# An eighth Strassen pair in each feed-forward layer, begun in the first half of the tokens

## The chip, the cores and the metric

The kernel runs on one core of one Trainium2 chip. The metric is the device time of one execution in microseconds (us); shorter is better. TensorE (PE) multiplies, VectorE (DVE) and ScalarE (ACT) do the element-wise work, GpSimd (POOL) does a little of it and issues transfers, and SyncE (SP) issues transfers only. PSUM, where PE accumulates, has eight banks of 128 partitions x 2 KB; one bank holds a 128 x 512 float32 tile.

## The reference

Two layers work on 512 tokens of width 1024. The first layer mixes tokens with causal average pooling, the second with causal differential attention. Each is followed by a SwiGLU feed-forward block (FFN) of width 2816. All arithmetic is float32.

```python
for i in range(DEPTH):                      # DEPTH = 2
    h = _multiscale_pool(x, ...) if i % 2 == 0 else _diff_attention(x, ...)
    x = _layernorm(ALPHA * x + h, ln_mix_g[i], ln_mix_b[i])
    x = _layernorm(ALPHA * x + _swiglu(x, w_gate[i], w_up[i], w_down[i]), ...)

def _swiglu(x, w_gate, w_up, w_down):
    return (jax.nn.silu(x @ w_gate) * (x @ w_up)) @ w_down
```

## The kernel before, in words

**A float32 product is three fast ones.** Each operand is split into a high part, a ScalarE cast to PE's faster type fp32r, and a low part, a VectorE subtraction of the high part from the value. PE then does high x high, high x low and low x high (`mm3`, lines 149 to 151). So each piece of weight costs a cast on ACT and a low part on DVE before PE can use it. x is kept transposed in `xt` as high and low parts: for each 128 tokens PE transposes (`pt`, line 235), ACT applies the norm's gain and bias and casts (lines 249 and 123), and DVE makes the low part (line 124). This is `turn(n, s)`, and it follows `norm(n, s)`, a short chain on DVE with one power on POOL (lines 183 to 208).

**Gate and up.** The 2816 columns are 22 blocks of 128. A weight row of the wall in DRAM is 128 x 1024 values, 512 KB, and gives one block of gate or of up. A plain block multiplies gate and up by all 1024 of x with 512 tokens as moving columns: 48 + 48 matmuls of 512 columns. The first `early` blocks (three in layer 0, two in layer 1) are computed in two token halves, 256 columns each, because the second half of x comes late: the loop over `lo = 0, 256` runs all early blocks for tokens 0 to 255, with the transposes of the last tokens between them (`late`), then all for tokens 256 to 511.

**Strassen pairs.** Blocks of number 2k and 2k+1 of this order are a pair k. The pairs of `SPLIT` (4 to 10) are done by Strassen's scheme in Winograd's form, two by two over gate/up and the halves of x and tokens: seven products of 24 matmuls with 256 columns (P1, Q5, P6, Q3, P7, P2, Q4) in place of eight. Their left sides are quarters of x and four sums of them (`xs`, made once per layer by `sums_of_x`, in steps called by `next(sums)`). Their right sides are four weight rows as they are or in sums of them (`sum` steps, line 636). The products go to three PSUM banks: A takes P1, P6, P7 and Q4 in one accumulation, C takes Q5 and Q3, B takes P2. After P1, ACT copies A's state to SBUF (`sg`); after P2, DVE adds bank B to it (line 925), and ACT applies Silu (line 932).

**What sets the order.** The order is written out by hand: each engine executes its instructions in the order of the code. `steps` lists cast, sum and low of each weight piece; `advance(upto)` and `ahead(upto)` emit steps until that piece is complete, a few pieces ahead of PE. Weight pieces lie in six slots of high and low part each (`w..h`/`w..l` or `g_..h`/`g_..l`) and start as raw rows in five buffers (`raws`), which SP fills in the order of the wall's rows. A slot is free when PE has done its last product on it. `weight_sums()` and `sum_hidden(k)` make sums for the down product, which is done by Strassen's scheme as well (lines 960 to 1000) and isn't touched. `ready(n)` emits cast and low of plain weight rows until n rows are ready, in and around attention.

Of the kernel before, what the change touches and what calls it, by code (L numbers as in the profile page):

```python
# [12 lines left out]
F32 = mybir.dt.float32  # L13
# [35 lines left out]
SPLIT = (4, 5, 6, 7, 8, 9, 10)  # L49
# [5 lines left out]
def trunk(ctx, tc, x, wall, pscale, lam_p, subln, table, lng, lnb, band, first, onehot, out):  # L55
# [37 lines left out]
    total = wall.shape[0]  # L93
    attn = 2 + 3 * FB
    vrow = {c: attn + 2 * c for c in range(4)}
    qrow = attn + 8
    order_of_rows = (
# [4 lines left out]
    rows_of_wall = list(range(total))  # L102
    rows_of_wall[attn : attn + 24] = order_of_rows
# [207 lines left out]
    with tc.tile_pool(name="pool", bufs=1) as pp:  # L311
# [198 lines left out]
        norm(0, 2)  # L510
        summed(3, 0, 1)
        spread_of(0, 3)
        ready(6)
# [19 lines left out]
    def ffn(layer, late):  # L533
# [3 lines left out]
        c1 = c0 + 2 * FB  # L537
        tt = nc.vector.tensor_tensor
        with tc.tile_pool(name=f"ffn{layer}", bufs=1) as fp:
# [12 lines left out]
            def block(i, b):  # L552

                if PAIRS[i][1] == 2:
                    return wall[c1 + 4 * i + b]
                return wall[c1 + 20 + b // 2][:, (b % 2) * 512 : (b % 2 + 1) * 512]
# [33 lines left out]
            chunks, index, steps = [], {}, []  # L590
# [7 lines left out]
            for k in range(HALF):  # L598
                j0 = index[k] = len(chunks)
                c = c0 + 4 * k  # L600
                if k in SPLIT:

                    chunks += [(c, ()), (c, (c, c + 1)), (c, (c, c + 2)), (c + 2, ())]
                    chunks += [(c + 1, (c + 1, c + 2)), (c + 3, ()), (c, (c, c + 3))]
                    step("cast", j0)
                    for w in (
                        "low 0, sum 1, cast 1, sum 4, cast 3, cast 4, low 1, sum 2, cast 2, low 3, "
                        "low 2, sum 6, cast 5, cast 6, low 4, low 5, low 6"
                    ).split(", "):
                        steps.append((w[:-2], j0 + int(w[-1])))  # L610
                else:
                    for i in range(4):
                        chunks.append((c + i, ()))
                        step("cast", j0 + i)
                        step("low", j0 + i)
# [115 lines left out]
            def load_terms(k):  # L731
                if k < HALF - 1:
                    c = c1 + 4 * (k // 2)
                    src = wall[c : c + 4][:, :, term_slice(k)].rearrange("(j r) p t -> p j r t", j=2)
                else:
                    src = wall[c1 + 20 : c1 + 22].rearrange("j p (r t) -> p j r t", r=2)
# [33 lines left out]
            def sum_hidden(k):  # L770

                first, second = hid[:, k, :256], hid[:, k, 256:]
                a12, a22 = hid[:, k + HALF, :256], hid[:, k + HALF, 256:]
                u = fp.tile([P, 2, 256], F32, tag="u", name=f"u{layer}_{k}", bufs=1)
                v = fp.tile([P, 2, 2, 256], F32R, tag="v", name=f"v{layer}_{k}", bufs=2)
# [7 lines left out]
                tt(v[:, :, 1, :], u, v[:, :, 0, :].bitcast(F32), op=ALU.subtract)  # L783
                yield
                nc.scalar.dma_start(out=ssum[:, :, :, k, :], in_=v.bitcast(F32))
# [41 lines left out]
            early = 3 if layer == 0 else 2  # L827
# [3 lines left out]
            sums = sums_of_x()  # L831
            ks = [range(4 * b, 4 * b + 4) for b in range(2)]
            by_part = [(0, 0, range(KB)), (0, 1, range(KB)), (1, 0, range(KB))]
            by_half = [(0, 0, ks[0]), (1, 0, ks[0]), (0, 0, ks[1]), (1, 0, ks[1])]
            by_half += [(0, 1, ks[1]), (0, 1, ks[0])]
            for lo in (0, 256):
                for f in range(early):
                    for i in range(2):
                        product(
                            accs[f][i], 2 * f + i, lo, lo + 256,  # L840
                            None if layer or lo else by_part if f or i else by_half,
                        )
                        if not lo and (f, i) in late:
                            late[f, i]()
                        if not lo:
                            advance(2 * early, True)
                    if lo:
                        advance(2 * f + 6)
                        gated(order[f], *accs[f])
                        affine(n - 1, f)  # L850
                        catch_up()
                        if f < 2:
                            weight_sums()
                            next(sums)
                        if f == 1:
                            behind.append(sum_hidden(0))

            def plain(f):
                k = f // 2
                j = index[k] + 2 * (f % 2)  # L860
# [10 lines left out]
                if f in (3, 5, 7):  # L871
                    weight_sums()
                if f == 3:
                    load_terms(3)
                if f % 2:
                    behind.append(sum_hidden(k))

            def strassen(k):
                names = {"P1": "A", "P6": "A", "P7": "A", "Q4": "A", "Q5": "C", "Q3": "C", "P2": "B"}
                banks = {b: bank(f"{b}{layer}_{k}") for b in "ACB"}  # L880
                lefts = {
                    "P1": [quarter(0, i, 0) for i in range(2)],
                    "P2": [quarter(0, i, 1) for i in range(2)],
                    "Q4": [quarter(1, i, 1) for i in range(2)],
                }
                for m, p in enumerate(("Q5", "P6", "P7", "Q3")):
                    lefts[p] = [xs[:, m, i] for i in range(2)]
# [3 lines left out]
                def both(t):  # L891
                    return t.rearrange("p (f t) -> p f t", f=2)
# [4 lines left out]
                for j, p in enumerate(GATE):  # L897
                    acc = banks[names[p]]
                    h, l = halves[index[k] + j]
                    xh, xl = lefts[p]  # L900
                    for f in range(2):
                        o = acc[:, f * 256 : (f + 1) * 256]
                        for kk in range(4):
                            c = slice((4 * f + kk) * P, (4 * f + kk + 1) * P)
                            for e, (w, x) in enumerate(((h, xh), (h, xl), (l, xh))):
                                nc.tensor.matmul(  # L906
                                    o, w[:, c], x[:, kk, :],
                                    start=p in ("P1", "Q5", "P2") and f + kk + e == 0,
                                    stop=p in ("Q4", "Q3", "P2") and (f, kk, e) == (1, 3, 2),
                                    skip_group_check=True,  # L910
                                )
# [17 lines left out]
                    ahead(index[k] + j + 6)  # L929
# [117 lines left out]
    def attention():  # L1047
        n = 2
        with tc.tile_pool(name="attn", bufs=1) as ap:
# [421 lines left out]
    ffn(0, {(1, 0): later(0, 2), (1, 1): later(0, 3)})  # L1471
# [110 lines left out]
```

## Time and profile before

| | us |
|---|---|
| median of 3 runs (939.54 to 940.16) | 939.98 |
| the profiled execution | 940.01 |
| its span on the core | 938.2 |
| PE busy | 925.0 |
| DVE busy | 789.8 |
| ACT busy | 512.9 |
| POOL busy | 126.7 |

The span runs from the first to the last instruction; times of rows are counted from its start. By the trace, x's first half is multiplied by the early blocks up to 52.0 us in layer 0, the second half from 52.0 to 69.3, plain blocks run to 123.7, Strassen pairs to 264.8 and the down product to 362.8. Attention follows to about 586. In layer 1 the early blocks' second half runs from 600.8 to 618.0, plain blocks to 683.3, and pairs to 824.5. In rows of instructions, a row has start, duration, engine, line, operation, out<-in, and in brackets the engine's idle time before it with what ended it.

### The profile page before, as it was taken

What the parts mean: (1) busy time and instruction counts of PE and PEld (TensorE: products, weight loads), DVE (VectorE), ACT (ScalarE), POOL (GpSimd) and SP (SyncE); (2) the same over time, 40 slices, a digit from 0 to 9 for tenths busy, and PEclk for the clock granted to TensorE, in tenths of its full rate; (3) what the DMA queues carried; (4) which work ended last, traced back from release to release, by engine and by line L of the source; (5) the groups of instructions that cost most, each with busy time, mean ns of one, the idle gap of its engine ahead of it and who ended that gap; (6) DMA issues with size and microseconds to landing.
All of it is one profiled execution on the core that took longest, in us unless ns stands there. A gap on an engine that the chain in (4) does not pass through costs nothing.

```text
span 938.2 us, 14939 instructions
## 1 busy us (share of the span) xinstructions
PE 925.0 (99%) x5710; PEld 827.2 (88%) x5710; DVE 789.8 (84%) x1166; ACT 512.9 (55%) x814; POOL 126.7 (14%) x152
## 2 busy tenths in 40 slices
PE   9999999999999999999999999999999999999996
PEld 8998899999988888888888887988899999988884
DVE  8969889999988778968888877788789999987678
ACT  6652444555564457667878754734245554654450
POOL 4221121110101201201112100211111110001101
PEclk9999999999999999999999999999999999999999
DMA  8487988886868988975666522597887885878942
GB/s 243 154 266 225 336 283 245 259 258 211 259 199 277 363 256 232 226 198 154 164 137 178 159 68 68 148 322 226 258 255 243 266 277 192 264 244 286 353 156 91
DMA packets 86038, 211.11 MB, mean 225 GB/s; under 512 B 15140, under 2 KB 26660, under 8 KB 85966
## 3 DMA queue, kind: packets, MB, share of 16 engines
q1 hardware_dynamic: 43420, 117.16, 38.1%
q0 software_dynamic: 18768, 58.20, 24.8%
q10 hardware_dynamic: 23778, 34.78, 10.4%
q8 instruction: 45, 0.74, 0.3%
q14 instruction: 27, 0.22, 0.1%
HBM read 173.40 MB, written 36.72 MB: 224 GB/s over the span
## 4 chain that ended last, share of the span: by engine, by line
PE 92%; DVE 5%; ACT 1%; issue 1%; DMA 0%; POOL 0%; DVEq 0%; ACTq 0%; POOLq 0%
PE A L906 17%; PE P L973 14%; PE C L906 9%; PE Q L973 6%; PE B L906 4%; PE g L150 3%; PE u L150 3%; PE g L149 3%; PE u L151 3%; PE u L149 3%; PE g L151 3%; PE s L1192 2%; PE va L1123 2%; PE wo L150 1%; PE wo L151 1%; PE q L149 1%
## 5 line engine op out<-in xcount | busy, mean ns | idle before, releaser
L636 DVE TENSOR_TENSOR raw<-raw,raw 128x1024 f32<-128x1024 f32 x56 | 68.3, 1219 | 0.5
L123 ACT CAST xs<-hid 128x512 fp32r<-128x512 f32 (+1 forms) x60 | 34.7, 581 | 24.4 <-DVE hid L813 24.4
L124 DVE TENSOR_TENSOR xs<-hid,xs 128x512 fp32r<-128x512 f32 (+1 forms) x60 | 38.5, 643 | 7.8 <-ACT xs L123 7.8
L1212 ACT ACTIVATE p<-p,mn 128x128 f32<-128x128 f32 (+3 forms) x64 | 35.2, 552 | 14.1 <-DVE mn L1207 14.1
L249 ACT ACTIVATE y<-pt,bT,gT 128x128 f32<-128x128 f32 x72 | 27.1, 456 | 26.6 <-PE pt L235 23.5
L744 POOL DMA_DIRECT2D b<-in_wall x20 | 14.0, 706 | 172.4 <-DMA tsum<-b 68.8
L805 POOL DMA_DIRECT2D xs<-ssum x24 | 17.4, 725 | 140.8 <-PE Q L973 67.8
L677 DVE TENSOR_TENSOR hid<-sg,u 128x512 f32<-128x512 f32 x16 | 11.0, 687 | 25.5 <-PE u L151 14.7
L199 POOL TENSOR_TENSOR rs<-rs,mhalf 128x1 f32<-128x1 f32 x16 | 12.8, 800 | 140.9 <-DVE rs L198 97.3
L744 POOL DMA_DIRECT2D hid<-in_wall x24 | 18.9, 831 | 77.5 <-DMA tsum<-hid 50.2
L1207 DVE CUSTOM_DVE_ANT_0 p<-s,bias 128x128 f32<-128x128 f32 (+3 forms) x64 | 28.0, 485 | 1.1 <-PE s L1192 1.1
L781 ACT CAST v<-u 128x512 fp32r<-128x512 f32 x22 | 13.7, 621 | 26.9 <-DVE u L779 26.8
L190 DVE BATCH_NORM_STATS2 st<-res 128x6 f32<-128x512 f32 x32 | 22.2, 694 | 1.1
L932 ACT ACTIVATE sg<-sg 128x512 f32<-128x512 f32 x14 | 8.9, 633 | 26.0 <-DVE sg L925 26.0
L745 POOL DMA_DIRECT2D hid<-in_wall x12 | 14.8, 1233 | 55.1 <-DMA hid<-in_wall 55.1
L693 ACT CAST xs<-hid 128x1024 fp32r<-128x1024 f32 x8 | 8.4, 1051 | 24.0 <-DVE hid L710 11.6
L124 DVE TENSOR_TENSOR xt<-y,xt 128x512 fp32r<-128x512 f32 x18 | 12.3, 691 | 10.9 <-ACT xt L123 10.7
L921 DVE TENSOR_TENSOR hid<-C,hid 128x512 f32<-128x512 f32 x14 | 9.7, 691 | 10.7 <-PE C L906 9.2
L1226 DVE SCALAR_TENSOR_TENSOR p<-p,sm,p 128x128 f32<-128x128 f32 (+3 forms) x32 | 17.6, 551 | 1.1
L917 ACT COPY hid<-C 128x512 f32<-128x512 f32 x14 | 8.2, 588 | 18.2 <-PE C L906 18.2
L124 POOL TENSOR_TENSOR sql<-sq,sqh 128x512 fp32r<-128x512 f32 x7 | 9.3, 1324 | 60.5 <-ACT sqh L123 60.5
L745 POOL DMA_DIRECT2D b<-in_wall x10 | 12.3, 1230 | 38.0 <-DMA b<-in_wall 38.0
(1211 smaller groups left out, 3637.1 us busy)
## 6 DMA issues: line engine op xcount, KB each, us to landing
raw<-in_wall SPq DMA_DIRECT2D x122, 512.0 KB, 5.0
r<-tsum SPq DMA_DIRECT2D x40, 512.0 KB, 4.5
hid<-in_wall POOLq DMA_DIRECT2D x36, 512.0 KB, 7.3
b<-in_wall POOLq DMA_DIRECT2D x30, 512.0 KB, 5.8
r<-in_wall SPq DMA_DIRECT2D x30, 512.0 KB, 4.5
tsum<-hid ACTq DMA_DIRECT2D x24, 512.0 KB, 5.4
ssum<-v ACTq DMA_DIRECT2D x22, 512.0 KB, 3.8
tsum<-b ACTq DMA_DIRECT2D x20, 512.0 KB, 4.9
```

The source lines that it names most:

```text
L123: nc.scalar.copy(dst_h, src)
L124: (low or nc.vector).tensor_tensor(dst_l, src, dst_h.bitcast(F32), op=ALU.subtract)
L149: nc.tensor.matmul(acc, ah, bh, start=start, stop=False)
L150: nc.tensor.matmul(acc, ah, bl, start=False, stop=False)
L151: nc.tensor.matmul(acc, al, bh, start=False, stop=stop)
L249: nc.scalar.activation(y[:, k, :], pt[:, k * P : (k + 1) * P], AF.Identity, bias=bT[:, n, kk : kk + 1], scale=gT[:, n, kk : kk + 1],)
L636: tt(t, raws[pair[0]], raws[pair[1]], op=ALU.add)
L744: nc.gpsimd.dma_start(out=t[:, j], in_=src[:, j])
L906: nc.tensor.matmul(o, w[:, c], x[:, kk, :], start=p in ("P1", "Q5", "P2") and f + kk + e == 0, stop=p in ("Q4", "Q3", "P2") and (f, kk, e) ...
L973: nc.tensor.matmul(accs[s], x[:, k, r], y[:, c], start=first and k == 0 and e == 0, stop=last and k == m - 1 and e == 2, skip_group_check= ...
L1207: nc.vector.tensor_tensor_reduce(out=p, in0=accs[c], in1=biases[h][:, w - 1 :: -1] if w < S else biases[h][:, ::-1], op0=ALU.add, op1=ALU. ...
L1212: nc.scalar.activation(p, p, AF.Exp, bias=mn[:, q, c : c + 1], scale=-1.0, accum_out=sm[:, q, c : c + 1],)
```

## The change

`SPLIT` gains pair 3, so that eight pairs are done by Strassen's scheme. `EARLY` is two blocks in layer 0 (three before) and one in layer 1 (two before). In the first token half, P1 and P2 of pair 3, which need only tokens 0 to 255, follow the early blocks; ACT copies P1 from bank A into a tile `g3`, and DVE adds bank B to it. Two rows of the wall, `pair` and `pair + 3`, are loaded early for this, and once more later for the pair's sums: two more loads of 512 KB per layer. Bank B is held for the whole layer. In later pairs ACT copies P1 from bank A into bank B, and P2 accumulates on it; the DVE addition is gone and Silu reads bank B. Further: one buffer `v` instead of two; `weight_sums` at other places; w5 is made ready ahead of the last norm of layer 0's mixer; the transpose of tokens 384 to 511 comes after P1 (after block 1's up before); the second half's first gate product of layer 0 takes x in halves; and in attention's end a `ready` stands ahead of `scaled(last)`.

```diff
-SPLIT = (4, 5, 6, 7, 8, 9, 10)
+SPLIT = (3, 4, 5, 6, 7, 8, 9, 10)
+EARLY = (2, 1)
...
+    def rows_of_ffn(layer, c):
+        g = list(range(c, c + 2 * FB))
+        e, pair = 2 * EARLY[layer], c + 4 * SPLIT[0]
+        return g[:e] + [pair, pair + 3] + g[e:] + list(range(c + 2 * FB, c + 3 * FB))
...
         norm(0, 2)
+        ready(6)
         summed(3, 0, 1)
         spread_of(0, 3)
-        ready(6)
         norm(0, 3)
...
+            def half_product(acc, j, left, start, stop):
+                h, l = halves[j]
+                xh, xl = left
+                for f in range(2):
+                    o = acc[:, f * 256 : (f + 1) * 256]
+                    for kk in range(4):
+                        c = slice((4 * f + kk) * P, (4 * f + kk + 1) * P)
+                        for e, (w, x) in enumerate(((h, xh), (h, xl), (l, xh))):
+                            nc.tensor.matmul(
+                                o, w[:, c], x[:, kk, :],
+                                start=start and f + kk + e == 0,
...
+            halved = [(w, e, ks[b]) for b in range(2) for w, e in ((0, 0), (1, 0), (0, 1))]
...
             for lo in (0, 256):
                 for f in range(early):
                     for i in range(2):
...
                     if lo:
-                        advance(2 * f + 6)
+                        advance(2 * f + 8)
                         gated(order[f], *accs[f])
                         affine(n - 1, f)
                         catch_up()
-                        if f < 2:
-                            weight_sums()
-                            next(sums)
+                        weight_sums()
                         if f == 1:
                             behind.append(sum_hidden(0))
+                if not lo:
+                    bankA, bankB = bank(f"A{layer}_{SPLIT[0]}"), bank(f"B{layer}")
+                    half_product(bankA, number[SPLIT[0], 0, "pair"], lefts["P1"], True, False)
+                    if "P1" in late:
+                        late["P1"]()
+                    nc.scalar.copy(both(g3), both(bankA))
+                    next(sums)
+                    half_product(bankB, number[SPLIT[0], 5, "pair"], lefts["P2"], True, True)
+                    tt(both(g3), both(bankB), both(g3), op=ALU.add)
+                    next(sums)
...
                     if p == "P1":
-                        g0 = tile_of(0)
-                        nc.scalar.copy(both(g0), acc)
+                        nc.scalar.copy(both(bankB), acc)
...
                     elif p == "P2":
-                        tt(both(g0), acc, both(g0), op=ALU.add)
+                        g0 = tile_of(0)
...
                     if p == "P2":
-                        nc.scalar.activation(g0, g0, AF.Silu)
+                        nc.scalar.activation(both(g0), acc, AF.Silu)
...
             for s in range(SB):
                 acc = gather(0, s, ws, between[s])
-                if s in (0, 3):
-                    scaled(last - 1 if s == 0 else last)
+                if s == 0:
+                    scaled(last - 1)
                 ready(cw + min(5 + s, WBUFS) if s < 3 else cw + 8)
+                if s == 3:
+                    scaled(last)
...
-    ffn(0, {(1, 0): later(0, 2), (1, 1): later(0, 3)})
+    ffn(0, {(1, 0): later(0, 2), "P1": later(0, 3)})
```

Three places show how it moves instructions. The first is the first token half of layer 0. On PE before, `u_1` (block 1's up) is followed by the transposes of the last 128 tokens and block 2 (`g_2`, `u_2`), whose weights are the pieces `g_4` and `g_5`; the high part's 16 matmuls come ahead of the low part's eight:

```order
L659 MATMUL u_1_538<-xt,w5h 128x256 x16
L659 MATMUL u_1_538<-xt,w5l 128x256 x8
L235 MATMUL pt_3_0_679<-ident,res 128x128 x4
L235 MATMUL pt_3_1_680<-ident,res 128x128 x4
L659 MATMUL g_2_539<-xt,g_4h 128x256 x16
L659 MATMUL g_2_539<-xt,g_4l 128x256 x8
```

On PE now, P1 of pair 3 (`A_3`) stands in the place of `g_2` and ahead of the transposes:

```order
L683 MATMUL u_1_538<-xt,w5h 128x256 x16
L683 MATMUL u_1_538<-xt,w5l 128x256 x8
L867 MATMUL A_3_678<-xt,g_4h 128x256 x2
L867 MATMUL A_3_678<-xt,g_4l 128x256
L867 MATMUL A_3_678<-xt,g_4h 128x256 x2
```

The last two lines go on by turns, 24 matmuls in all; then come the transposes and P2 (`B_679`, from `g_5`). The low part of `g_4` is wanted at the third matmul, where it was wanted at the seventeenth.

On DVE at the same place before, `w5l` stands behind the last tokens' sums, and `g_4l` behind their norm:

```order
L124 TENSOR_TENSOR w4l<-raw_326,w4h 128x1024
L208 TENSOR_SCALAR res<-res,mv_2_492,rs_2_494 128x1024
L183 SCALAR_TENSOR_TENSOR res<-res,mix_0_400 128x512
L190 BN_STATS st_3_505<-res 128x6
L183 SCALAR_TENSOR_TENSOR res<-res,mix_1_401 128x512
L190 BN_STATS st_3_505<-res 128x6
L196 BN_AGGR mv_3_509<-st_3_505 128x2
L198 TENSOR_SCALAR rs_3_511<-mv_3_509 128x1
L124 TENSOR_TENSOR w5l<-raw_328,w5h 128x1024
L208 TENSOR_SCALAR res<-res,mv_3_509,rs_3_511 128x1024
L642 TENSOR_TENSOR g_4l<-raw_330,g_4h 128x1024
```

On DVE now:

```order
L133 TENSOR_TENSOR w4l<-raw_326,w4h 128x1024
L217 TENSOR_SCALAR res<-res,mv_2_492,rs_2_494 128x1024
L133 TENSOR_TENSOR w5l<-raw_328,w5h 128x1024
L192 SCALAR_TENSOR_TENSOR res<-res,mix_0_400 128x512
L199 BN_STATS st_3_511<-res 128x6
L192 SCALAR_TENSOR_TENSOR res<-res,mix_1_401 128x512
L199 BN_STATS st_3_511<-res 128x6
L205 BN_AGGR mv_3_515<-st_3_511 128x2
L207 TENSOR_SCALAR rs_3_517<-mv_3_515 128x1
L217 TENSOR_SCALAR res<-res,mv_3_515,rs_3_517 128x1024
L666 TENSOR_TENSOR g_4l<-raw_330,g_4h 128x1024
```

`w5l` has moved ahead of the sums, and all from the sums to `g_4l` behind it.

The second place is ACT after the last transposed tokens of layer 0 (`y_3_1`). Before, the table of Silu is loaded and the first Silu (`sg_0`, block 0's gate) stands ahead of the casts of the next weights:

```order
L123 CAST xt<-y_3_1_696 128x4x128
L676 ACT_TABLE_LOAD
L676 ACTIVATE sg_0_799<-g_0_535 128x512
L639 CAST g_6h<-raw_497 128x1024
L639 CAST g_7h<-raw_514 128x1024
L639 CAST g_8h<-raw_571 128x1024
L676 ACTIVATE sg_11_870<-g_1_537 128x512
```

Now:

```order
L132 CAST xt<-y_3_1_721 128x4x128
L915 COPY g_0_545<-A_3_678 128x512
L663 CAST g_6h<-raw_497 128x1024
L663 CAST g_7h<-raw_504 128x1024
L663 CAST g_8h<-raw_570 128x1024
L700 ACT_TABLE_LOAD
L700 ACTIVATE sg_0_819<-g_0_535 128x512
```

The copy of P1 and three casts now stand ahead of the first Silu.

The third place is the end of attention on DVE, where the last head's output is scaled (`rso`, then its low part into `xt`) and the output product's weights are made. Before:

```order
L183 SCALAR_TENSOR_TENSOR res<-res,wo_2_0_5792 128x512
L183 SCALAR_TENSOR_TENSOR res<-res,wo_2_1_5793 128x512
L1277 SCALAR_TENSOR_TENSOR rso_5856<-o_5812,gcol,rso_5856 128x512
L124 TENSOR_TENSOR xt<-rso_5856,xt 128x512
L124 TENSOR_TENSOR w98l<-raw_5518,w98h 128x1024
L124 TENSOR_TENSOR w99l<-raw_5650,w99h 128x1024
```

Now, where all numbers of weights are two higher:

```order
L192 SCALAR_TENSOR_TENSOR res<-res,wo_2_0_5827 128x512
L192 SCALAR_TENSOR_TENSOR res<-res,wo_2_1_5828 128x512
L133 TENSOR_TENSOR w100l<-raw_5553,w100h 128x1024
L133 TENSOR_TENSOR w101l<-raw_5685,w101h 128x1024
L1327 SCALAR_TENSOR_TENSOR rso_5891<-o_5847,gcol,rso_5891 128x512
L133 TENSOR_TENSOR xt<-rso_5891,xt 128x512
```

Two weights' low parts stand ahead of the scaling instead of behind it.

More of the change, by code (lines that the diff above doesn't have):

```diff
@@ L92, in trunk @@
     divided = [0]
-    total = wall.shape[0]
     attn = 2 + 3 * FB
@@ L536, in ffn @@
         c0 = base[0]
-        c1 = c0 + 2 * FB
+        c1 = c0 + 2 * FB + 2
+        down = rows_of_wall[c0] + 2 * FB
+        early = EARLY[layer]
         tt = nc.vector.tensor_tensor
@@ L596, in step, with plain_chunk @@
                     steps.append((kind, j))
[L598 to L615, printed above, removed]
+            def plain_chunk(key, c):
+                number[key] = len(chunks)
+                chunks.append((c, ()))
+                step("cast", number[key])
+                step("low", number[key])
@@ L835, in ffn @@
             by_half += [(0, 1, ks[1]), (0, 1, ks[0])]
+            halved = [(w, e, ks[b]) for b in range(2) for w, e in ((0, 0), (1, 0), (0, 1))]
+            g3 = fp.tile([P, S], F32, name=f"g3_{layer}")
+            ready_first = 2 * early + 2
             for lo in (0, 256):
@@ L879, in strassen @@
                 names = {"P1": "A", "P6": "A", "P7": "A", "Q4": "A", "Q5": "C", "Q3": "C", "P2": "B"}
[L880 to L887, printed above, removed]
+                begun = k == SPLIT[0]
@@ L888, in strassen @@
+                banks = {"A": bankA if begun else bank(f"A{layer}_{k}"), "C": bank(f"C{layer}_{k}")}
+                banks["B"] = bankB
                 rows = hid[:, k : k + HALF + 1 : HALF, :]
                 first, second = rows[:, :, :256], rows[:, :, 256:]
-                def both(t):
-                    return t.rearrange("p (f t) -> p f t", f=2)
                 def tile_of(i):
                     return keep.tile([P, S], F32, tag="y", name=f"sg{layer}_{k}_{i}", bufs=2)
-                for j, p in enumerate(GATE):
-                    acc = banks[names[p]]
[L899 to L911, printed above, removed]
@@ new lines, in strassen @@
+                for m, p in enumerate(GATE):
+                    if begun and p in ("P1", "P2"):
+                        if p == "P2":
+                            g0 = g3
+                            nc.scalar.activation(g0, g0, AF.Silu)
+                        continue
+                    acc = banks[names[p]]
+                    j = number[k, m, "pair"]
+                    half_product(
+                        acc, j, lefts[p], p in ("P1", "Q5"), p in ("Q4", "Q3", "P2")
+                    )
```

74 lines of the change are left out of this document (57 added, 17 removed).

## The prediction

> **What bounds the kernel now.** The page comes first: the span, the engines' busy time, and the chain that ended last.
>
> ```profile
> span 938.2 us, 14939 instructions
> PE 925.0 (99%) x5710; PEld 827.2 (88%) x5710; DVE 789.8 (84%) x1166; ACT 512.9 (55%) x814; POOL 126.7 (14%) x152
> ```
>
> PE is busy 925.0 of 938.2 us. So the time is PE's work plus what makes it wait. The next view is PE's waits, with total, count and longest.
>
> ```profile
> PE u L659 <- DVE w5l L124: 0.8, 1, 0.8
> PE wo L150 <- DVE w98l L124: 0.7, 1, 0.7
> PE pt L235 <- DVE res L208: 0.2, 1, 0.2
> ```
>
> Two of these lie where the change acts. No wait on a DMA is listed. The windows by stage come third: length, then busy time of PE, weight load, DVE, ACT and POOL, granted clock, DMA share, GB/s.
>
> ```profile
> 46.00:52.00 6.00, 6.00 (x53) 6.00 (x52) 3.23 (x5) 3.91 (x10) 0.00 (x0) 1.00 0.98 355
> 52.00:69.20 17.20, 17.20 (x146) 17.20 (x145) 11.40 (x12) 8.25 (x10) 5.41 (x6) 1.00 0.85 230
> 69.20:123.70 54.50, 54.50 (x243) 45.12 (x243) 48.13 (x56) 18.42 (x22) 9.34 (x10) 1.00 0.85 279
> 143.90:264.80 120.90, 120.90 (x1009) 120.90 (x1009) 114.36 (x140) 63.65 (x82) 10.45 (x12) 1.00 0.79 248
> 600.00:623.00 23.00, 23.00 (x174) 22.12 (x173) 15.93 (x17) 12.54 (x19) 5.42 (x6) 1.00 0.99 305
> 925.00:930.00 5.00, 4.19 (x19) 3.14 (x17) 5.00 (x9) 0.00 (x0) 0.67 (x1) 1.00 0.28 105
> 930.00:938.20 8.20, 0.00 (x0) 0.00 (x0) 4.21 (x8) 0.00 (x0) 0.92 (x1) 0.73 0.35 129
> ```
>
> PE fills every stage of the FFN. DVE has 5.80 us idle in the second row and 6.37 in the third, 12.2 together, and only 5% in the pairs (fourth). The sum is made against the profiled execution's 940.01 us, which is 0.03 above the median.
>
> **1. PE's work.** The chain of waits gives the matmuls' prices (start, us, what).
>
> ```profile
> 49.13 2.88 PE u L659 x24
> 52.01 0.12 PE g L149
> 69.29 0.23 PE g L149
> 123.72 2.87 PE A L906 x24
> ```
>
> From 52.01 to 69.29 lie six products of 24 matmuls with 256 columns: 17.28 / 144 = 0.120 us each. From 69.29 to 123.72 lie 240 with 512 columns: 0.2268 each. In layer 0, 288 + 240 matmuls stand ahead of pair 4. Afterwards: two early blocks in halves (192 small), two plain blocks (192 large), pair 3 (168 small). That is 72 small more and 48 large fewer: 8.64 - 10.89 = -2.25 us. Layer 1 goes from 192 + 288 to 264 + 240, the same -2.25. Together **-4.5**.
>
> The Trainium skill, page "TensorE: Matmul & The Clock Gate", section "Back-to-back issue gap", gives N / 2.4 + 2.5 ns for a warm gap, which is 109 and 216 ns here. The trace has 120 and 227, about 11 ns above it at both sizes. By the page each layer would gain 2.50, and the sum would end 0.5 lower; the rows decide.
>
> **2. Layer 0, first token half.** DVE's and PE's timelines round the wait on `w5l` (start, duration; in brackets the idle time before and its cause):
>
> ```profile
> 39.50 0.68 DVE L183 SCALAR_TENSOR_TENSOR res<-res,mix 128x512 f32<-128x512 f32 x1
> 42.58 1.23 DVE L124 TENSOR_TENSOR w5l<-raw,w5h 128x1024 fp32r<-128x1024 f32 x1
> 44.24 0.81 DVE L208 TENSOR_SCALAR res<-res,mv,rs 128x1024 f32<-128x1024 f32 x1 [0.44 <-POOL rs L199]
> 44.97 1.22 DVE L642 TENSOR_TENSOR g_4l<-raw,g_4h 128x1024 fp32r<-128x1024 f32 x1
> 46.11 1.22 DVE L642 TENSOR_TENSOR g_5l<-raw,g_5h 128x1024 fp32r<-128x1024 f32 x1
> ```
> ```profile
> 40.87 2.15 PE L659 MATMUL u<-xt,w5h 128*128 128x256 f32 x16
> 43.86 1.21 PE L659 MATMUL u<-xt,w5l 128*128 128x256 f32 x8 [0.83 <-DVE w5l L124]
> 45.20 1.06 PE L235 MATMUL pt<-ident,res 128*128 128x128 f32 x8
> 46.02 1.19 PE L659 MATMUL g<-xt,g_4h 128*128 128x256 f32 x8
> ```
>
> `w5l` moves to 39.50, so u runs unstalled from 40.87 to 43.75. What stood there comes one low part later, 46.11 - 44.97 = 1.14: the norm at 45.38, `g_4l` from 46.11 to 47.33. P1 follows u at once, does two matmuls and waits at the third for `g_4l`, from 43.99 to 47.37, 3.38 us. Before, `g_4l` was covered by transposes and 16 high matmuls. P1's other 22 end at 50.01, the transposes (45.20 to 46.02) 0.82 later, P2 at 53.71. The second half, at 52.01 before, so starts 1.70 later, and layer 0 keeps -2.25 + 1.70 = **-0.55**. Within P1 the stall lies between 0 (`g_4l` there when P1 starts) and 3.38 plus the 1.14 of one more low part.
>
> The last tokens' x is next in line, since its transposes now follow P1. Before, from ACT's first operation on them to DVE's last low part it took 52.28 + 0.69 - 48.03 = 4.94 us:
>
> ```profile
> 48.03 1.51 ACT L249 ACTIVATE y<-pt,bT,gT 128x128 f32<-128x128 f32 x4 [3.09 <-DVE xt L124]
> 52.28 0.69 DVE L124 TENSOR_TENSOR xt<-y,xt 128x512 fp32r<-128x512 f32 x1 [1.37 <-ACT xt L123]
> ```
>
> With the first transposes done at 50.4 the last low part is there at about 55.4. The second half's first product now takes x in halves, the low part of the second half in its last four matmuls, at 53.71 + 20 x 0.12 = 56.1. So it is in time by 0.7 us, and I count zero for it; one more half-size DVE operation ahead of it (0.60) would still cost nothing.
>
> **3. VectorE up to the end of pair 3 in layer 0.** The new work is three more low parts (pair 3 has seven pieces for four), four sums, and about four half-size operations (bank B to `g3`, Q3, P7, a product more), less Silu's partner products. Prices by start-to-start times:
>
> ```profile
> 102.73 1.22 DVE L696 TENSOR_TENSOR xs<-hid,xs 128x1024 fp32r<-128x1024 f32 x1
> 103.86 0.69 DVE L783 TENSOR_TENSOR v<-u,v 128x512 fp32r<-128x512 f32 x1
> 104.46 1.22 DVE L642 TENSOR_TENSOR g_15l<-raw,g_15h 128x1024 fp32r<-128x1024 f32 x1
> ```
>
> Large operations take 1.14, half-size 0.60. 7 x 1.14 + 4 x 0.60 = 10.4 us, against the 12.2 idle. It fits with 1.8 us over, if the idle time can be used. Its largest piece before, and ACT at that time:
>
> ```profile
> 57.87 0.69 DVE L677 TENSOR_TENSOR hid<-sg,u 128x512 f32<-128x512 f32 x1 [4.90 <-PE u L151]
> ```
> ```profile
> 54.93 0.60 ACT L676 ACTIVATE sg<-g 128x512 f32<-128x512 f32 x1 [1.39 <-PE g L151]
> 55.43 1.04 ACT L639 CAST g_6h<-raw 128x1024 fp32r<-128x1024 f32 x1
> 57.69 1.05 ACT L639 CAST g_7h<-raw 128x1024 fp32r<-128x1024 f32 x1 [1.23 <-PE u L150]
> ```
>
> The 4.90 was spent waiting for block 0's up while the casts waited for PE to free slots. Now casts of `g_6` and `g_7` stand ahead of the first Silu, in the slots that P1 and P2 free at 50.01 and 53.71. Their low parts fill that hole. Cost **0**, with bounds 0 and +2.7 (rival A). If Q3's weight is the tight one, the margin is that 1.8.
>
> **4. Attention's end.** PE waits there for `w98l`:
>
> ```profile
> 567.08 0.75 DVE L1277 SCALAR_TENSOR_TENSOR rso<-o,gcol,rso 128x512 f32<-128x512 f32 x1 [2.67 <-ACT rso L1272]
> 568.52 0.69 DVE L124 TENSOR_TENSOR xt<-rso,xt 128x512 fp32r<-128x512 f32 x1 [0.69 <-ACT xt L123]
> 569.60 0.40 PE L149 MATMUL wo<-w98h,xt 128*128 128x512 f32 x1
> 570.75 0.50 PE L150 MATMUL wo<-w98l,xt 128*128 128x512 f32 x1 [0.75 <-DVE w98l L124]
> ```
>
> Two matmuls 1.15 apart instead of 0.227: 0.92 lost. Two low parts moved into DVE's 2.67 us of idle time take 2.28 and remove that wait. The scaled head is next in line: its low part in `xt` was there at 568.52 + 0.69 = 569.2, and the first matmul on it is at 569.60. The 0.2 that a later transpose waits for the norm grows a little as PE comes earlier, 0.15 by my estimate. **-0.75**, bounds -0.92 and 0 (casts too late on ACT, so that rso slips).
>
> **5. Layer 1.** P1 and P2 take the place of block 1's halves, with the same 48 matmuls and two weights made by a cast and a low part, in the same order. No wait is listed there before. DVE's idle time is 7.07 us from 600 to 623, and 11.9 in the plain blocks behind it:
>
> ```profile
> 623.00:683.30 60.30, 60.30 (x269) 49.93 (x268) 48.41 (x57) 20.05 (x24) 9.34 (x10) 1.00 0.82 253
> ```
>
> That is 19.0 against the same 10.4, where layer 0 has 12.2. The gain of -2.25 stays; its bounds are 0 and +2.7 as in layer 0, with 0 nearer by that slack.
>
> **6. Bank B, the other moves.** In 14 later pairs DVE loses one addition of 0.69, ACT's copy goes to PSUM instead of SBUF. DVE isn't on the path in the pairs (no wait listed), so nothing is gained. No row shows a copy by ACT into PSUM; the nearest is its copy from PSUM into SBUF, 0.588 us:
>
> ```profile
> L917 ACT COPY hid<-C 128x512 f32<-128x512 f32 x14 | 8.2, 588 | 18.2 <-PE C L906 18.2
> ```
>
> P2 wants the bank only after the four products Q5, P6, Q3 and P7, which take 11.5 us (2.88 each), so that even a copy ten times as long would be hidden.
>
> Holding bank B takes a bank from the plain blocks, whose five others turn over once in 2.5 blocks of 21.8 us / 2. One buffer `v` for two is asked for once per pair, 20 us. The four more row loads are rival B. If DVE got late in the pairs, the 0.69 taken off per pair would bring it back: 8 x 0.69 over a layer. All of these count zero.
>
> **Sum.** -0.55 (layer 0) - 0.75 (attention) - 2.25 (layer 1) = -3.55: **936.5 us**.
>
> **Rivals.** A: VectorE is late at pair 3. If the hole of 4.90 us can't be filled, since slots come free too late, 10.4 meets 7.3, and Q3 waits some 2.7 in layer 0 and perhaps a little in layer 1: 939.2, no change that can be told. For it: DVE is at 95% in the pairs and can't catch up. Against it: the casts' new place. Chance 0.18.
>
> B, slower: loads become the bound. Each layer reads 1.05 MB more, and right behind the early blocks, where the DMA share is 0.98 to 0.99. At 305 GB/s that is 3.4 us per layer, 6.9 in all: 943.4. Against it: no wait of PE names a DMA, and casts were released by PE. It decides where a raw row lands after its slot is free. Chance 0.14.
>
> C: the clock. The stall of 3.38 us is PE's longest. In this trace the granted clock falls only at the end: PE's last work ends at about 929.2, and the clock is still 1.00 in the window to 930 and 0.73 in that of 8.20 us behind it, so half speed for at most 4.4 us (0.27 x 8.2 x 2) from about 933.8, 4.6 us after. A fall at P1 would double the matmuls until it rises; if for as long as the stall, half of 3.38 us, +1.7: 938.2; two such windows 939.9. The Trainium skill's page named above, section "Part 1: The HAM clock gate (the "warmup" mystery)", says that a free-running idle window of about 3.4 us throttles PE to half; by that rule P1 is on the edge, while the trace's one fall came later. Chance 0.08.
>
> D: P1 doesn't stall much, -1.7 to -3.4 more, about 934.0. That `g_4l` is wanted at P1's third matmul speaks against it. Chance 0.10.
>
> **How the numbers follow.** My case has 0.50 and 936.5. About 0.2%, 1.9 us, is what can be told from no change: faster lies below 938.1, slower above 941.9. Faster: my case 0.47, D 0.10, C 0.03, A 0.05 = 0.65. Same: A 0.11, C 0.05, my case 0.03 = 0.19. Slower: B 0.14 and a heavy A 0.02 = 0.16. The range leaves out half of B and of D and goes from 934.5 to 942.0.
>
> **What would show it.** Right: PE waits once at P1's third matmul, about 3.4 us, on `g_4l`; none on `w5l` or the output product's weight; the second half of layer 0 starts at about 53.7, pair 4's P1 at 123.2 (A, line 906 before); 0.2 at most on weights in pair 3. Wrong: a wait at Q3 or P6 of pair 3 on DVE (A), waits of casts on DMA (B), a granted clock under 1.0 before 60 us (C), a span shorter still with no wait on `g_4l` (D), or a wait in the pairs for the copy into bank B, which the sum leaves out.

## The result and the profile after

The changed kernel takes 954.77 us (median of 5 runs, 954.43 to 955.83) against 939.98 before: ratio 1.0158, 95% interval 1.0145 to 1.0172. It is slower by 14.8 us where 3.5 less were forecast. The profiled execution took 954.77 us. The page's first lines and the waits of PE that bear on the change:

```profile
span 953.0 us, 15072 instructions
PE 925.6 (97%) x5758; PEld 831.5 (87%) x5758; DVE 801.3 (84%) x1172; ACT 521.2 (55%) x826; POOL 126.1 (13%) x152
```
```profile
PE A L867 <- DVE hid L973: 14.7, 2, 7.3
PE A L867 <- DVE g_4l L666: 2.3, 1, 2.3
PE pt L244 <- DVE res L217: 0.2, 1, 0.2
```

The first row is new: twice, once in each layer, PE waits 7.3 us at bank A for VectorE's line 973. That line is `tt(second, second, acc, op=ALU.subtract)`, VectorE's read of bank A after P7. The waits on `w5l` and on the output product's weight are gone. PE's busy time should have fallen by the work saved, yet it rose by 0.6: a busy PE isn't PE at full speed. The windows behind the three waits show the granted clock (third number from the end, ahead of DMA share and GB/s):

```profile
46.60:49.90 3.30, 3.30 (x15) 3.30 (x16) 2.25 (x3) 0.00 (x0) 0.45 (x1) 0.51 0.92 297
49.90:53.30 3.40, 3.40 (x32) 3.40 (x31) 0.00 (x0) 1.89 (x5) 2.27 (x3) 1.00 1.00 322
128.60:132.60 4.00, 4.00 (x22) 4.00 (x23) 2.76 (x3) 0.57 (x1) 0.00 (x0) 0.60 0.91 274
693.90:698.30 4.40, 4.37 (x20) 4.38 (x21) 2.84 (x3) 0.63 (x1) 0.02 (x1) 0.50 0.98 309
```

After each of them the clock was at 0.50 to 0.60 for 3.3 to 4.4 us; the second row shows it back at 1.00. The places in time come from the chain of waits. Before:

```profile
586.67 0.97 PE pt L235 x8
824.45 14.99 PE P L973 x66
```

After:

```profile
46.57 4.34 PE A L867 x22
51.78 2.87 PE B L867 x24
128.55 7.43 PE A L867 x48
135.98 2.88 PE C L867 x24
595.10 0.94 PE pt L244 x8
693.93 7.97 PE A L867 x48
840.14 14.99 PE P L1023 x66
```

Layer 0's second token half starts at 54.65 (51.78 + 2.87) instead of 52.01: +2.64. Pair 4's P1, the second half of the 48 matmuls from 128.55, starts at 133.10 (135.98 - 2.88) instead of 123.72: +9.38. Attention's last transposes stand at +8.43, so attention won back 0.95. The down product of layer 1 stands at +15.69, so layer 1 lost 7.26. The tail gives back 0.9, and the span is 14.8 longer. In parts:

| | layer 0 | layer 1 |
|---|---|---|
| PE's work, as forecast | -2.25 | -2.25 |
| P1's stall, less the stalls it replaces (what remains of +2.64) | +0.94 | |
| half clock behind it: 22 matmuls in 4.34, not 2.64 | +1.70 | |
| wait at Q4 for the read of P7 | +7.33 | +7.33 |
| half clock behind it: 48 matmuls, not 5.76 | +1.67 | +2.21 |
| sum (measured) | +9.39 (+9.38) | +7.29 (+7.26) |

Why the read is late is seen on PE and DVE around it in layer 0:

```profile
120.94 0.28 PE L867 MATMUL A<-xs,g_17l 128*128 128x256 f32 x1
128.55 0.80 PE L867 MATMUL A<-xt,g_18h 128*128 128x256 f32 x2 [7.33 <-DVE hid L973]
```
```profile
119.55 2.48 DVE L660 TENSOR_TENSOR raw<-raw,raw 128x1024 f32<-128x1024 f32 x2
121.95 1.22 DVE L666 TENSOR_TENSOR g_20l<-raw,g_20h 128x1024 fp32r<-128x1024 f32 x1
123.08 0.68 DVE L971 TENSOR_TENSOR hid<-C,hid 128x512 f32<-128x512 f32 x1
123.69 1.22 DVE L660 TENSOR_TENSOR raw<-raw,raw 128x1024 f32<-128x1024 f32 x1
124.82 1.22 DVE L666 TENSOR_TENSOR g_22l<-raw,g_22h 128x1024 fp32r<-128x1024 f32 x1
126.06 1.23 DVE L666 TENSOR_TENSOR g_21l<-raw,g_21h 128x1024 fp32r<-128x1024 f32 x1
127.21 0.68 DVE L807 TENSOR_TENSOR v<-u,v 128x512 fp32r<-128x512 f32 x1
127.81 0.68 DVE L973 TENSOR_TENSOR hid<-hid,A 128x512 f32<-128x512 f32 x1
```

P7 ends at 121.2. Its read stands in VectorE's queue behind sums and low parts of pair 4 (`g_20` to `g_22`), which PE wants only later, and comes at 127.81. Q4 accumulates on the same bank A, so it must not start before the read. In all other pairs P2 stands between P7 and Q4 and gives the read 2.88 us; in pair 3 P2 was done in the first token half.

### The profile page after: what moved, and what is told of

Same layout as the page of the kernel before. It is cut to its first block, busy times and chain, and to the rows that moved or that the text cites. A ratio compares the mean times of both kernels' runs of the same rounds, so it can differ in the third digit from the quotient of the medians.

```text
span 953.0 us, 15072 instructions
## 1 busy us (share of the span) xinstructions
PE 925.6 (97%) x5758; PEld 831.5 (87%) x5758; DVE 801.3 (84%) x1172; ACT 521.2 (55%) x826; POOL 126.1 (13%) x152
## 4 chain that ended last, share of the span: by engine, by line
PE 82%; DVE 12%; issue 3%; ACT 2%; DMA 0%; POOL 0%; DVEq 0%; ACTq 0%; POOLq 0%
PE A L867 19%; PE P L1023 13%; PE C L867 8%; PE Q L1023 6%; PE B L867 5%; PE va L1173 2%; PE s L1242 2%; PE q L158 2%; PE q L160 2%; PE k L158 2%; PE k L160 2%; PE q L159 2%; PE k L159 2%; DVE raw L660 2%; PE vc L1173 1%
## 5 line engine op out<-in xcount | busy, mean ns | idle before, releaser
L660 DVE TENSOR_TENSOR raw<-raw,raw 128x1024 f32<-128x1024 f32 x64 | 78.1, 1221 | 1.0
L768 POOL DMA_DIRECT2D b<-in_wall x20 | 14.0, 706 | 183.7 <-DMA tsum<-b 122.5
L867 PE MATMUL A<-xt,g_18h 128*128 128x256 f32 x32 | 9.3, 392 | 14.7 <-DVE hid L973 14.7
L978 ACT ACTIVATE sg<-A 128x512 f32<-128x512 f32 x16 | 9.6, 597 | 24.9 <-PE A L867 24.9
L867 PEld LDWEIGHTS A<-xt,g_18h 128*128 128x128 f32 x32 | 7.7, 294 | 15.1 <-DVE hid L973 15.1
L769 POOL DMA_DIRECT2D hid<-in_wall x12 | 14.8, 1233 | 41.8 <-DMA hid<-in_wall 41.8
L701 DVE TENSOR_TENSOR hid<-sg,u 128x512 f32<-128x512 f32 x12 | 8.2, 684 | 12.5 <-PE u L160 7.3
```

The costliest lines, as they stand in the source:

```text
L660: tt(t, raws[pair[0]], raws[pair[1]], op=ALU.add)
L867: nc.tensor.matmul(o, w[:, c], x[:, kk, :], start=start and f + kk + e == 0, stop=stop and (f, kk, e) == (1, 3, 2), skip_group_check=True,)
```

## The experiments

Two theories were held against each other. Theory 1, order: P2 is missing between P7 and Q4, and the read queues behind steps for later products. Theory 2, amount: VectorE has more to do up to pair 4 than fits, so that whatever order is mended, the wait shows elsewhere.

**Reads first** (the first kernel). In pair 3 the steps behind P6 and Q3 are put off until behind P7.

```diff
+                late_steps = [0]
...
+                    if begun and p in ('P6', 'Q3'):
+                        late_steps[0] += 1
+                        continue
                     ahead(j + 6)
-                    catch_up()
+                    for _ in range(1 + (late_steps.pop() if p == "P7" and begun else 0)):
+                        catch_up()
```

> The changed kernel, but in pair 3 of both layers the weight steps and side work that stand behind P6 and Q3 come only behind P7, so that VectorE's reads of Q3 and of P7 stand right behind each other. VectorE's work in total is the same. Theory 1 (order: Q4 accumulates on bank A, VectorE must read P7 out of it first, P2 no longer stands between them, and that read waits in VectorE's queue behind steps for later pairs): the two waits of 7.3 us fall to about 0.7 each, the clock stays at 1.00 there, and 2 x 6.6 + 1.7 + 2.2 = 17 us are saved: about 937.7. Theory 2 (VectorE simply has too much work up to pair 3): the deferred steps are then late for pair 4's products, the waits move there, and the time stays near 954.

Measured: 947.02 us, 7.8 less than the change, not 17. The waits of PE:

```profile
PE A L867 <- ACT B L966: 5.9, 2, 3.0
PE A L867 <- DVE g_4l L666: 2.3, 1, 2.3
PE A L867 <- DVE hid L974: 1.6, 2, 0.8
```

The read's wait fell to 0.8 as theory 1 said. But 3.0 per layer came back at pair 4's P6, which accumulates on bank A and waits for ScalarE's copy of P1: that copy now queues behind casts that wait for VectorE's sums. About half the loss went with this order; the other half came back at another place.

**High part first** (the second kernel), for layer 0's P1 alone:

```diff
+                if high_first:
+                    for i, (w, x) in enumerate(((h, xh), (h, xl), (l, xh))):
+                        for f in range(2):
+                            for kk in range(4):
...
```

> The changed kernel, but layer 0's P1 of pair 3 does its 16 products with the weight's high part first and the 8 with its low part last. By the theory that the stall of 2.29 us at its third matmul comes from that order, and that the half clock behind it comes from the stall: the wait falls to about 0.7, the matmuls behind it run at 0.12 us instead of 0.20, and 1.6 + 1.7 = 3.3 us are saved: about 951.5. If the clock falls for another reason, 1.6 are saved: 953.2. If pair 3's VectorE wait takes up what PE gains (its end there is set by VectorE alone), nothing is saved: 954.8.

Measured: 953.15 us, 1.6 less; the profiled spans differ by 2.8 (950.2 against 953.0). The stall fell to 0.6 and the clock stayed at 1.00 there:

```profile
43.00:52.00 9.00, 8.38 (x71) 8.18 (x70) 5.99 (x9) 5.57 (x15) 4.64 (x6) 1.00 0.86 314
```

The 1.6 us of the median are what was expected if the clock fell for another reason. The trace, of the fastest of the four runs, decides against that: the order of parts made the stall, and the stall made the half clock. The two waits of 7.3 us stayed.

**Both together** (the third kernel), and, apart from that, **only the steps behind Q3 put off**:

> Both edits together. If they are independent: 954.8 - 17 - 3.3 = 934.4, faster than the kernel before by 0.6%. If VectorE's total work is the bound, near 951.

> As the first, but only the steps behind Q3 are put off, not those behind P6. VectorE's read of P7 then comes at once behind its read of Q3, which itself is 5 us late: by theory 1 the wait is about 3.3 us (7.33 less sum, two low parts and v, 4.1) in each layer, 8.2 saved in two. On the clock: if a stall of 3.3 us halves it as one of 2.29 did, the half clock behind it stays (946.5); if not, 942.7.

Measured: 945.30 and 946.28 us. Both together has the waits of the first kernel (0.8 and 3.0 per layer), with 0.6 in place of 2.3 on `g_4l`. With only Q3's steps put off the read's wait is 3.2, where 3.3 was expected, and no new wait appears:

```profile
PE A L867 <- DVE hid L974: 6.4, 2, 3.2
```

That kernel is as fast as those in which the read's wait is 0.8. What is gained at the read beyond this is lost behind it, as theory 2 says.

**Pair 4's P1 ahead of Q4**, as a cover in P2's place, with the reads first; and the same without putting steps off:

```diff
                     elif p == "P7":
                         tt(second, second, acc, op=ALU.subtract)
+                        if begun:
+                            nextA.append(bank(f"A{layer}_{k + 1}"))
+                            half_product(
+                                nextA[0], number[k + 1, 0, "pair"], lefts["P1"], True, False
+                            )
+                            nc.scalar.copy(both(bankB), both(nextA[0]))
...
```

> The third kernel (reads first, high part first), with pair 4's P1 and ScalarE's copy of it moved ahead of pair 3's Q4, and ahead of the steps put off, so that 2.88 us of products stand between P7 and Q4 as P2 does in other pairs, and the copy into bank B doesn't queue behind casts. By theory 1 both waits that the third kernel kept (0.8 on VectorE's read, 3.0 on ScalarE's copy, in each layer) go, and the half clock behind the 3.0 with them: from about 945 to about 936. By theory 2 (too much VectorE work in this stretch) a wait for a low part of pair 4 of about 3 us per layer takes their place, and the time stays over 942.

> The second kernel (high part first) with pair 4's P1 ahead of Q4, but with the steps behind P6 and Q3 left where the change put them: VectorE's read of P7 stays 6.7 us late and gets 2.88 us of cover. By theory 1 each wait falls from 7.3 to about 4.5, 5.8 saved; the clock still dips: about 947. If the read came later because PE runs on (VectorE being the bound), the waits stay near 7 and the time near 953.

Measured: 947.22 and 946.51 us. In the first the waits moved once more, to pair 4's Q3, behind ScalarE's copy of Q5; in the second they are 4.45, 7.33 less the 2.88 of cover, as theory 1 said:

```profile
PE C L879 <- ACT hid L986: 7.1, 2, 3.5
PE A L879 <- DVE g_21l L666: 0.9, 2, 0.5
```
```profile
PE A L879 <- DVE hid L991: 8.9, 2, 4.5
```

In the five kernels in which something was moved ahead of or behind the read, 3.2 to 4.5 us per layer remain. That speaks for theory 2, and the next experiments test it.

**The addition back on VectorE.** Bank B's part of the change is undone in pairs 4 to 10, on the first of these two:

```diff
-                        nc.scalar.copy(both(bankB), acc)
+                        nc.scalar.copy(both(g0), acc)
...
+                        tt(both(g0), acc, both(g0), op=ALU.add)
```

> As the first of this call, but in pairs 4 to 10 the bank-B part is undone: ScalarE copies P1 to SBUF, P2 starts bank B, VectorE adds it, as before. It prices that part by itself: VectorE gets 14 additions of 0.60 us back. If VectorE isn't on the path in the pairs, 0 +- 0.5 us against the first; if VectorE's lateness at pair 4 decides, up to 0.6 per pair until it has caught up, 1 to 3 us.

Measured: 947.68 us (947.60 to 948.29) against 947.22 (944.34 to 948.09), with the same waits of 3.5 and 0.5. Nothing can be told apart: no gain from the 14 additions less on VectorE can be seen.

**A lighter stretch.** Work is moved out of VectorE's stretch ahead of pair 4, with nothing left out:

```diff
-                    if f >= 3:
+                    if 2 * f + i >= 5:
                         next(sums, None)
...
-                if f % 2:
+                if f % 2 and f < 5:
                     weight_sums()
...
-                if f % 2:
+                if f % 2 and f < 5:
                     behind.append(sum_hidden(k))
...
+                    if second_pair and p == "P6":
+                        behind.append(sum_hidden(2))
...
+                if k == 5:
+                    weight_sums()
```

It was put on four kernels: the one with reads first and pair 4's P1 ahead, the one with both first edits, the one with pair 4's P1 ahead and late reads, and the one with the high part first alone.

> The kernel with pair 4's P1 ahead of Q4, with VectorE's side work taken out of the stretch ahead of pair 4 and done elsewhere, nothing left out: the weight sum of block 5 (1.4 us) goes to pair 5's end, the hidden sum of pair 2 (2.2 us) into pair 4, and one step of x's sums (2.3 us) comes half a block earlier: 5.9 us less in front of pair 4. Theory 2 (VectorE has some 4 us too much there once the order is mended): the waits of 3.5 and 0.5 us per layer go, and the time falls from 947 to about 937. If the wait on ScalarE's copy has a cause of its own in ScalarE's queue, it stays near 3 us and the time above 943.

> The same relief on the third kernel, without pair 4's P1 ahead of Q4: the waits of 0.8 on VectorE's read of P7 stay (PE ends P7 and needs the read at once), those of 3.0 on ScalarE's copy into bank B go if VectorE's work behind it decides: 945.3 - 5.9 - the half clock behind it, about 938; 2 x 0.8 over the other kernel of this call.

> High part first, pair 4's P1 ahead of Q4, the relief of 5.9 us, and the steps behind P6 and Q3 where the change put them, so that VectorE has no reason to idle in pair 3. The wait on its read of P7 was 4.45 us per layer with pair 4's P1 between; with 5.9 us less work ahead of it, theory 2 (in that stretch VectorE's amount of work decides) expects none: 946.5 - 8.9 - some 3.5 of half clock = 934, faster than the kernel before by 0.6%. If another queue takes over, as it did when the steps were put off, a wait of 2 to 3 us per layer shows on ScalarE and the time is about 941.

> High part first and the relief alone: Q4 still follows P7 at once, steps where the change put them. The wait of 7.3 us per layer falls by the 5.9 taken out ahead of the read, to about 1.4 (not under 0.7, the read itself): 953.15 - 11.8 - some 3 of half clock = 938. If the relief doesn't come through (VectorE waits elsewhere for casts instead), the waits stay over 4 and the time over 946.

Measured: 947.30, 945.76, 937.24 and 947.71 us. The first two missed. With the steps put off, VectorE now ran out of work in pair 3 (idle 1.2 and 2.1 us ahead of its two reads in the first, 0.8 and 2.1 in the second) and was late again afterwards. In the second, PE waits 1.2 us for ScalarE's copy into bank B and 2.0 at pair 4's Q4, in each layer. In the first, ScalarE's copy of Q5 stood behind the issue of a store that waited for VectorE:

```profile
129.22 3.97 ACTq L779 DMA_DIRECT2D tsum<-b  x2
133.23 0.58 ACT L986 COPY hid<-C 128x512 f32<-128x512 f32 x1 [3.02 <-DMA tsum<-b]
```

The third, with steps left where the change put them, has no wait left in pair 3:

```profile
span 934.5 us, 15098 instructions
PE 921.5 (99%) x5758; PEld 826.7 (88%) x5758; DVE 801.2 (86%) x1172; ACT 520.6 (56%) x826; POOL 126.1 (13%) x152
```
```profile
PE A L879 <- DVE hid L991: 2.0, 3, 0.8
PE A L867 <- DVE g_4l L666: 0.6, 1, 0.6
```

At 937.24 (936.29 to 940.24, 10 runs) it is 0.3% faster than the kernel before, 940.32 in 13 runs beside it: ratio 0.9973, interval 0.9963 to 0.9982. The fourth keeps a wait of 2.9 per layer at Q4 (2.88 and 2.87), where 1.4 was expected, and took 947.71, where 938 was. It also waits 0.8 at pair 4's Q4, as the third does. Its four runs lie at 944.8, 945.2, 950.2 and 950.4; the trace is of the 945.2, and what made the last two longer isn't shown.

The four kernels without steps put off read as an account: 7.33 with neither edit, 4.45 with P1 as cover, 2.9 with the lighter stretch, none with both. But the 2.9 are not work that is still too much. The chain of waits of the fourth kernel, and VectorE's rows there:

```profile
115.32 2.77 PE A L879 x23
118.12 1.05 ACT g_21h L663
119.23 1.11 issue
120.34 0.69 DVE hid L986
121.08 7.51 PE A L879 x48
```
```profile
119.20 1.23 DVE L666 TENSOR_TENSOR g_21l<-raw,g_21h 128x1024 fp32r<-128x1024 f32 x1 [0.28 <-ACT g_21h L663]
120.34 0.68 DVE L986 TENSOR_TENSOR hid<-hid,A 128x512 f32<-128x512 f32 x1
```

VectorE had caught up and was idle for 0.28 us. It waited for ScalarE's cast `g_21h`, which goes into the slot of P7's own weight and so began at P7's end, 118.12. Cast, low part and read follow one another, and Q4 starts 2.88 after P7. This is order again: the read stands behind a low part that can't come before P7's end. In layer 1 the rows are the same (cast at 680.46, Q4 at 683.41). So the lighter stretch took away the whole 4.45 that VectorE was late, and the cover hides the chain of 2.88. That the two add up to 7.33 is no check: one product happens to take as long as that chain. Both theories hold, each for its part.

**One wait more.** In the kernel of 937.24, 0.8 us per layer remain at pair 4's Q4, behind the hidden sum that was moved there. It was started one product later:

```diff
-                    if second_pair and p == "P6":
+                    if second_pair and p == "P7":
                         behind.append(sum_hidden(2))
```

> The kernel of 937.2 with one thing more: pair 2's hidden sum (four operations, 1.6 us), which there stands ahead of VectorE's read of pair 4's P7 and makes Q4 of pair 4 wait 0.81 us in each layer, starts one product later, behind that read. By theory 1 both waits go: 1.6 saved, 935.6. By VectorE's amount of work they come back at another read of pair 4 or 5, and the time stays at 937.2.

Measured: 953.30 us, against either expectation. The two waits are gone (0.3 left), and two of 7.8 and 7.6 came:

```profile
149.31 0.52 ACTq L809 DMA_DIRECT2D ssum<-v  x1
159.47 0.62 ACT L805 CAST v<-u 128x512 fp32r<-128x512 f32 x1 [9.96 <-DMA ssum<-v]
160.00 0.58 ACT L987 COPY hid<-A 128x512 f32<-128x512 f32 x1
```

Pair 2's hidden sum now runs into pair 4's. With one buffer `v` the second sum's cast waits 9.96 us until the first one's store has read the buffer; the copy of pair 5's P6 stands behind that cast on ScalarE, and PE's P7 behind the copy. The chain is read from the trace; no kernel with two buffers was run.

## Why the prediction was wrong

**PE's work** was right: layer 1 closes with -2.25 in the account above (in layer 0 one row was fitted, so it is no check). A plain block is 24 + 24 matmuls of 512 columns, not the 48 + 48 of the text on the kernel before, and the 192 large matmuls are four plain blocks, not two; the counts and the sum are right.

**Layer 0, first half.** The mechanism was right: `w5l` came at 39.55, u ran without a stall, P1 stalled at its third matmul on `g_4l`. The stall was 2.29, not 3.38. The norm stood at 44.57, not 45.38, since POOL's power took 0.55 us here and 1.41 in the row from which it was shifted. So P1 went on 0.80 earlier than forecast (46.57, not 47.37). The cost was higher all the same, since the half clock added 1.70: 1.70 - 0.80 + 1.70 = 2.60 of the +2.64 measured. That was rival C, given 0.08 as an alternative and not counted in the sum. That its price of 1.7 was met is luck: it let the clock fall for as long as a stall of 3.38, and it fell for about as long behind a stall of 2.29.

**VectorE up to the end of pair 3**, counted at zero, is the step that failed, in layer 0 and, as part 5, in layer 1. Its amount of work was about right: VectorE's busy time rose by 11.5 us with 14 additions less, whose return added 7.6 in the experiment. So some 19.1 were added, 9.6 per layer, against 10.4 forecast. Two things were wrong. It held that all idle time ahead of pair 3 can be used. In layer 0 the hole of 4.90 us was filled as forecast, but 5.0 us stayed idle from 54.65 to 108. In layer 1 more did:

```profile
620.00:640.00 20.00, 20.00 (x92) 16.65 (x91) 16.04 (x20) 6.46 (x9) 3.88 (x4) 1.00 0.99 330
640.00:680.00 40.00, 40.00 (x198) 33.97 (x197) 34.56 (x37) 13.72 (x16) 5.40 (x6) 1.00 0.70 198
680.00:700.00 20.00, 12.67 (x90) 12.47 (x89) 16.89 (x21) 6.68 (x10) 2.72 (x3) 0.83 0.89 283
```

VectorE had 9.4 us idle from 620 to 680 and PE still waited 7.33 of the 20 us behind. The idle time lies where the steps written in the code are done, and `ahead` allows only so many pieces ahead of PE. The second thing: it asked only when each weight is needed (Q3 and P6), where the wait came from a read: it never asked what stands between P7 and Q4 on bank A once P2 is gone. Rival A named VectorE at pair 3 rightly, but at the wrong instruction, and at 2.7 (its own 10.4 less 7.3 is 3.1) for what cost 7.33 and a half clock, twice.

**Attention's end**: -0.75 forecast, -0.95 measured, and the wait named is gone. **Bank B**: counted zero; undoing it showed nothing that can be told, and ScalarE's copy into PSUM takes 0.582 us (14 copies) where 0.588 was used. **One buffer `v`**: zero as forecast in the changed kernel, but its cover is the distance between two hidden sums, and the last experiment shows a wait of 9.96 us without it. **Rival B**, the loads: no wait of PE on a DMA appears in the changed kernel, and none of the experiments needed it. Loads were not varied by themselves. **Rival D** didn't come.

The forecast's own sum, 936.5, is near the 937.24 of the kernel in which the read has its cover and VectorE its relief. In part that is luck: this kernel has the high part first as well, so that layer 0's second token half starts at 51.39, where the forecast had 53.71, and it still waits 0.8 per layer at pair 4. The forecast was missed by 14.8 + 3.5 = 18.3 us, five times the gain.

## What to carry to other kernels

When a product is taken out of a sequence, ask whose read of an accumulator it covered. In these kernels the next product on bank A had to wait for VectorE's read of it, and the read had to wait its turn among the steps written ahead of it, up to 7.33 us. Ask also whether one of those steps waits for the very product that is read: with all backlog gone, such a step still held the read back by 2.88. Compare idle time with added work only inside the window in which the order of the code lets that work be done; the mean over a stage says nothing about it. Put short reads that free a bank ahead of work for later, but leave no hole in the busy engine, since work put off came back here as the next wait.

## What was not expected of the hardware

PE's clock fell to half after stalls much shorter than the one before the clock's fall at the end of the kernel before (some 4.6 us). After P1's stall of 2.29 us it was at 0.51 for 3.3 us in the changed kernel. Over the window from 43 to 52 us it was at 0.81 there, and at 0.81 and 0.82 in the two other kernels that kept that stall. Stalls of 0.6 to 1.2 never did it. Behind stalls of 2.0 to 3.5 us it differed within one execution. In the second of the lighter kernels, a wait of 2.0 at pair 4's Q4 left the clock at 1.00 in layer 0 and was followed by 0.64 from 705.3 to 710 us in layer 1. With the same wait of 3.5 us in both layers, the kernel with pair 4's P1 ahead of Q4 and reads first kept its clock in layer 0 and lost it in layer 1:

```profile
105.00:145.00 40.00, 35.76 (x286) 34.79 (x285) 37.26 (x45) 17.63 (x24) 6.63 (x7) 1.00 0.84 267
675.00:710.00 35.00, 30.99 (x244) 30.59 (x243) 32.06 (x39) 16.60 (x22) 5.41 (x6) 0.95 0.90 286
```

The Trainium skill, page "TensorE: Matmul & The Clock Gate", section "Part 1: The HAM clock gate (the "warmup" mystery)", speaks of a free-running window of about 3.4 us. That the same stall falls on either side fits a free-running window; that stalls of 2.0 and 2.29 us sufficed does not fit its length, and the measurement decides. In the account above a stall cost its length and 1.7 to 2.2 us more. Four runs of the kernel with pair 4's P1 ahead and reads first went from 944.34 to 948.09, but seven of the kernel before beside them went from 939.39 to 942.67, so that the scatter isn't shown to come from such stalls.
